# Experts taken in the order of their token counts, three of them with 64 slots and their weights standing

## Chip, cores and metric

One core of a Trainium2 chip runs the kernel. The time is device microseconds of one execution, the median of several. The parts of the core that matter here are TensorE (matmuls, with a weight load ahead of each), VectorE (DVE), ScalarE (ACT), the SP queue that issues the transfers from HBM, and 16 DMA engines that carry them out.

## What is computed

A stack of eleven mixing and feed-forward stages on 256 tokens of width 1024, and last a layer of eight routed experts and a norm. The experts, cut from the reference:

```python
def moe_swiglu(h, w_router, wg, wu, wd):
    xt = h.reshape(-1, d)                       # 256 x 1024
    logits = (xt @ w_router).astype(jnp.float32)
    top_v, top_i = lax.top_k(logits, TOP_K)     # 2 of 8
    gates = jax.nn.softmax(top_v, axis=-1)
    comb = jnp.sum(jax.nn.one_hot(top_i, N_EXPERTS) * gates[..., None], axis=1)
    y = jnp.zeros_like(xt)
    for e in range(N_EXPERTS):
        y = y + comb[:, e:e + 1] * swiglu(xt, wg[e], wu[e], wd[e])
    return y

def swiglu(x, wg, wu, wd):                      # 1024 x 3584, 1024 x 3584, 3584 x 1024
    return (jax.nn.silu(x @ wg) * (x @ wu)) @ wd
```

## The kernel before, in words

Weights come from HBM in raw tiles of 128 x 2048 floats (1 MiB), by `load` (line 431), one transfer on the SP queue each. `conv_w` (line 457) makes two halves of a tile and splits each half into two parts of a rounded type (fp32r): ScalarE casts the raw half to `whi` (line 462), VectorE subtracts it from the raw half and writes `wlo` (line 463). There are four buffers each of `whi` and `wlo` (`W_BUFS`), and 13 raw tiles in this stage (`RAW_BUFS` 4, `MORE_RAW` 6 and 3). Activations are split in the same way, and a product of two split operands is three matmuls (hi x hi, lo x hi, hi x lo), all issued by the helper `mm` (line 326).

`moe_stage` (line 1780) routes: VectorE finds each token's two experts, matmuls count the tokens ahead of each in its expert, and `sel` holds, for each token and expert, its slot counted from one, or zero. `rest` (line 1833) computes the gates `comb` and the largest count, later. Then `moe_round` (line 1877) runs over the eight experts in the order of their numbers. The tokens of an expert have 128 slots; if one has more than 128 tokens, a second round (line 1858) does the remaining ones.

`places` (line 1878) is called for a pair of experts: it compares slot numbers with `iota` to get the 0/1 matrix `pm`, and gathers the normed input of both experts by 32 matmuls (`mpg`), split into `gh` and `gl`. The first pair is gathered at the start, the others in group 3 of the odd experts. `places_back` (line 1904) transposes `pm` for the way back, in group 4 of each expert.

An expert runs over seven groups of 512 hidden columns (`NG`). In a group, `up` (line 1918) takes two raw tiles of `moe_g` and two of `moe_u`. The gathered tokens stand (`gh`, `gl`, a 128 x 128 block each) and the weights stream, 512 columns in a matmul: for gate (`eg`) and up (`eu`) 8 blocks of the input by three matmuls each. ScalarE takes the SiLU of `eg`, VectorE multiplies by `eu`, and `turn` (line 1939) transposes the 128 x 512 result by four TensorE transposes (`ept`) and splits it into `eah` and `eal`. `down` (line 1947) takes two raw tiles of `moe_d`; the turned activations stand, the weights stream, three matmuls of 512 columns for each of four blocks and two halves of the output (`eacc`). The down of a group is issued behind the up of the next one, and the turn between its gate and its up. After seven groups `back` (line 1963) weights the rows by their gates and scatters them to the tokens. The tile framework orders the instructions of each engine when the program is built; at run time each engine's queue is in order.

Of the kernel before, what the change touches and what calls it, by code (L numbers as in the profile page):

```python
# [10 lines left out]
F32 = mybir.dt.float32  # L11
# [18 lines left out]

STAGES = ["ssm", "xa0", "ffn0", "cf", "xa1", "ffn1", "ab", "cd", "hy0", "sw", "hy1", "moe", "final"]


# ---------------------------------------------------------------- host layout
# [196 lines left out]
# ---------------------------------------------------------------- device program  # L231
# [14 lines left out]
def hybrid_stack_kernel(ctx: ExitStack, tc: tile.TileContext, A, out, voff, coff, stages=STAGES):  # L246
# [5 lines left out]
    # the tiles of the stages; before the routed experts they make room for more raw weights  # L252
# [43 lines left out]
    # ---- allocation helpers  # L296
    def rotating(tag, shape, dt, name):
        # by turns in the pools that hold tiles of this kind
        c = turns[tag]
        i = c[0] % sum(n for _, n in c[1])  # L300
        c[0] += 1
        for pool, n in c[1]:
            if i < n:
                return pools[pool].tile(list(shape), dt, tag=tag, name=name, bufs=n)
            i -= n
# [7 lines left out]
    def g4(name, shape, dt=F32):  # L313
        return pools["attn" if "attn" in pools else "work"].tile(list(shape), dt, tag="g4", name=name, bufs=6)
# [16 lines left out]
    def early(name, shape, dt=F32, pool="work"):  # L331
        # kept until its pool ends
        return pools[pool].tile(list(shape), dt, tag="k_" + name, name=name, bufs=1)

    # ---- persistent data
# [17 lines left out]
    # constants used as they come, and those that are converted first  # L353
# [66 lines left out]
    # ---- weights  # L420
# [3 lines left out]
    def behind(insts):  # L424
        # keep what is traced inside from being issued before these
# [40 lines left out]
    def load_last(name, i):  # L466
        # in smaller steps, as nothing follows that could hide them
# [64 lines left out]
    def square_step(q, acc, m):  # L532
        # squares of the outputs as they end, and sums of the earlier ones
# [15 lines left out]
    class OutProj:  # L549
# [15 lines left out]
        def feed(self, hi, lo):  # L565
# [13 lines left out]
            if self.k == self.nk:  # L579
                # the two that come last lie in different banks  # L580
# [6 lines left out]
    # ---- norms  # L587
# [6 lines left out]
    def rsqrt(o, v):  # L594
        # o = v ** -0.5: a first guess from the bits of v, good to 3.5%, a step
        # of third order to 2.5e-5, and a Newton step to 1e-9
# [19 lines left out]
    def col_sums(o, parts, first=True, last=True):  # L616
        # sums over the partitions, one token per row: o [P, 2]
# [6 lines left out]
    def spread(o, c, start=False):  # L624
        # a value per token, from rows to every partition of o [., T]
# [21 lines left out]
    class Norm:  # L647
        # the input of a stage: gain times x in two parts; the root mean
        # square is known later and goes on what the products give
# [190 lines left out]
    def stack_hl(rows, n, dst):  # L840
        # rows: psum [n, W] -> dst [64, W] with the two parts on rows 0.. and 32..
# [3 lines left out]
    # ---- state-space mixer  # L845
    def ssm_stage():
# [20 lines left out]
        # time steps  # L867
# [25 lines left out]
        # minus the running sums; the first chunk's also as seen from the second  # L893
# [107 lines left out]
    # ---- cross attention  # L1001
# [126 lines left out]
    # ---- gated MLPs  # L1128
# [51 lines left out]
    # ---- convolution module  # L1180
    def cf_stage():
# [7 lines left out]
        def gate(w, o):  # L1189
            for b in range(2):  # L1190
# [7 lines left out]
                # twice the gated value; the halves are taken back below  # L1198
# [3 lines left out]
        def taps_pe(n):  # L1202
            # some of the taps, as products with diagonal matrices
# [82 lines left out]
    # ---- self attention on heads of 64  # L1286
    def head_stats(tiles, h):
        # tiles: [P, n, T], two heads on the partitions of each
# [17 lines left out]
    def head_scale(tiles, nq, gq, gk, st):  # L1306
        # unit-norm heads in place; both gains and the scale go on the keys
# [92 lines left out]
    def run_heads(n, score, turn, out, fill=(), a=LEAD):  # L1400
        # three steps per head, each behind the next head's earlier ones
# [16 lines left out]
    def ab_stage():  # L1418
# [3 lines left out]
        for part in range(2):  # L1422
# [5 lines left out]
            if part == 0:  # L1428
                # forget gate: negative log and its running sum
# [39 lines left out]
            def bias(hd):  # L1469
                def f(p):  # L1470
# [3 lines left out]
                    # the running sums are of the negated logs  # L1474
# [20 lines left out]
    def cd_stage():  # L1495
        h = begin()
        # differential half
# [62 lines left out]
        # sliding window half: query tile t holds heads t and t + 4  # L1560
# [65 lines left out]
    # ---- gated convolution and linear recurrence  # L1626
    def hybrid_stage(l):
# [6 lines left out]
        # the gate comes as half of one plus a tanh  # L1634
# [46 lines left out]
        # recurrence  # L1681
        ybs = []
        ss, la_, bb = [], [], []
        for i in range(4):
# [7 lines left out]
            # 1 - a^2 = -tanh(log a) (1 + a^2)  # L1692
# [394 lines left out]
```

## Time and profile before

| | |
|---|---|
| median of 3 runs | 2751.4 us (2750.27 to 2752.5) |
| span of the profiled execution | 2753.1 us |
| TensorE matmuls, busy | 2697.2 us, 98% of the span |
| weight loads, busy | 2398.0 us, 87% |
| VectorE, busy | 2201.6 us, 80% |
| ScalarE, busy | 1728.4 us, 63% |
| read from HBM | 616.04 MB, 224 GB/s over the span |
| expert tiles read | 112 of each of gate and up, and of down, 1 MiB each |

The span reaches from the first to the last instruction of one profiled execution; the times are of executions without the profiler, and the two differ by 1.7 us. Busy time of TensorE is modelled: matmuls overlap in the array, so the step from one start to the next is the better measure of what one costs. A weight load (PEld) has a duration of its own and runs beside the matmul before it. "Idle before" and the waits name what ended an engine's wait.

### The profile page before, as it was taken

The numbers are of one execution on the slowest core, as the hardware profiler recorded it, in microseconds if no ns is written. First come the engines' busy times: TensorE is split into PE (matmuls) and PEld (weight loads), VectorE is DVE, ScalarE is ACT, GpSimd is POOL, SyncE is SP. The second block draws the span as 40 slices with busy tenths as digits, with TensorE's granted clock in tenths as the row PEclk, the third lists the DMA queues.
The fourth block names the chain that finished last, engine by engine and source line by source line (L and its number), as shares of the span: only waits on it lengthen the run. The fifth ranks groups of instructions, "written<-read, shape, count | busy, mean of one in ns | idle before, by whom it ended". The sixth has DMA issues, their size and how long they took to land. (4 is left out here: it accounts for less than half of the span.)

```text
span 2753.1 us, 44558 instructions
## 1 busy us (share of the span) xinstructions
PE 2697.2 (98%) x17440; PEld 2398.0 (87%) x17440; DVE 2201.6 (80%) x3344; ACT 1728.4 (63%) x2563; POOL 7.7 (0%) x76
## 2 busy tenths in 40 slices
PE   8999999999999999999999999999999999999997
PEld 8799999999889988888999999888887878787876
DVE  8787597798668776767875577999998888888887
ACT  6665465565656555555654455877777777777776
POOL 0000000000000000000000000000000000000000
PEclk9999999999999999999999999999999999999999
DMA  7145445433435543342655554999999999999993
GB/s 260 62 169 184 138 155 189 162 108 123 169 117 190 184 145 127 113 139 100 260 198 184 184 177 169 347 363 351 351 343 343 339 349 359 349 344 343 362 343 115
DMA packets 87259, 620.05 MB, mean 225 GB/s; under 512 B 9936, under 2 KB 10064, under 8 KB 12800
## 3 DMA queue, kind: packets, MB, share of 16 engines
q1 hardware_dynamic: 86608, 616.57, 62.3%
q8 instruction: 138, 2.26, 0.3%
q14 instruction: 81, 0.66, 0.1%
q10 hardware_dynamic: 432, 0.56, 0.1%
HBM read 616.04 MB, written 1.05 MB: 224 GB/s over the span
## 5 line engine op out<-in xcount | busy, mean ns | idle before, releaser
L463 DVE TENSOR_TENSOR wlo<-raw,whi 128x1024 fp32r<-128x1024 f32 (+1 forms) x1164 | 1390.1, 1219 | 343.3 <-ACT whi L462 335.5
L462 ACT CAST whi<-raw 128x1024 fp32r<-128x1024 f32 (+1 forms) x1164 | 1195.6, 1049 | 573.8 <-PE wv L326 296.4
L326 PE MATMUL wv<-hh,whi 128*128 128x256 f32 x2400 | 681.2, 285 | 14.7 <-ACT hh L661 13.4
L326 PE MATMUL wv<-hl,whi 128*128 128x256 f32 x2400 | 680.1, 284 | 0.1
L326 PE MATMUL wv<-hh,wlo 128*128 128x256 f32 x2400 | 677.0, 283 | 1.6 <-DVE wlo L463 1.5
L326 PEld LDWEIGHTS wv<-hh,whi 128*128 128x128 f32 x2400 | 456.4, 190 | 18.7 <-ACT hh L661 14.6
L326 PEld LDWEIGHTS wv<-hh,wlo 128*128 128x128 f32 x2400 | 455.7, 190 | 4.1 <-DVE wlo L463 3.2
L326 PEld LDWEIGHTS wv<-hl,whi 128*128 128x128 f32 x2400 | 456.9, 190 | 1.8 <-DVE hl L662 0.7
L326 PE MATMUL eg<-wlo,gh 128*128 128x512 f32 x448 | 178.5, 398 | 2.8 <-DVE wlo L463 2.8
L326 PE MATMUL eu<-whi,gh 128*128 128x512 f32 x448 | 179.5, 401 | 0.0
L326 PE MATMUL eu<-wlo,gh 128*128 128x512 f32 x448 | 177.7, 397 | 1.4 <-DVE wlo L463 1.3
L326 PE MATMUL eg<-whi,gh 128*128 128x512 f32 x448 | 178.3, 398 | 0.0
L326 PE MATMUL eg<-whi,gl 128*128 128x512 f32 x448 | 177.2, 395 | 0.0
L326 PE MATMUL eacc<-whi,eal 128*128 128x512 f32 x448 | 177.1, 395 | 0.0
L326 PE MATMUL eacc<-whi,eah 128*128 128x512 f32 x448 | 177.0, 395 | 0.0
L326 PE MATMUL eu<-whi,gl 128*128 128x512 f32 x448 | 177.0, 395 | 0.0
L326 PE MATMUL eacc<-wlo,eah 128*128 128x512 f32 x448 | 162.6, 400 | 0.0
L326 PE MATMUL acc<-fl,whi 128*128 128x256 f32 x576 | 161.7, 281 | 0.0
L326 PE MATMUL acc<-fh,wlo 128*128 128x256 f32 x576 | 161.1, 280 | 0.0
L326 PE MATMUL acc<-fh,whi 128*128 128x256 f32 x576 | 160.6, 279 | 0.0
L837 DVE SCALAR_TENSOR_TENSOR cv<-pad,vec,cv 128x256 f32<-128x256 f32 x288 | 124.8, 479 | 1.4 <-ACT cv L834 0.6
L326 PEld LDWEIGHTS acc<-fl,whi 128*128 128x128 f32 x576 | 108.2, 188 | 0.3 <-DVE fl L478 0.3
(539 smaller groups left out, 4302.6 us busy)
## 6 DMA issues: line engine op xcount, KB each, us to landing
raw<-moe_u SPq DMA_DIRECT2D x112, 1024.0 KB, 7.1
raw<-moe_g SPq DMA_DIRECT2D x112, 1024.0 KB, 7.1
raw<-moe_d SPq DMA_DIRECT2D x111, 1024.0 KB, 7.0
raw<-ffn_in SPq DMA_DIRECT2D x44, 1024.0 KB, 5.0
raw<-sw_in SPq DMA_DIRECT2D x28, 1024.0 KB, 5.0
raw<-ffn_out SPq DMA_DIRECT2D x22, 1024.0 KB, 5.0
raw<-hy_in SPq DMA_DIRECT2D x20, 1024.0 KB, 5.0
raw<-ssm_in SPq DMA_DIRECT2D x18, 1024.0 KB, 5.2
```

The costliest lines, as they stand in the source:

```text
L326: return pe.matmul(o, l, r, start=start, stop=stop, skip_group_check=True)
L462: act.copy(hi[:, cs], raw[:, cs])
L463: dve.tensor_sub(lo[:, cs], raw[:, cs], f32v(hi[:, cs]))
L837: dve.scalar_tensor_tensor(y, pad[:, j, 4 - s : 4 + T - s], taps[i], y, op0=OP.mult, op1=OP.add)
```

## The change

- In `rest`, VectorE ranks experts 1 to 7 by their counts (expert 0 is given the first place by a large addend), writes the order into `idx`, and carries `sel`, the counts and `comb` over into that order (`selp`, `cp`, `combp`).
- Positions 0 to 7 take the ranks 0, 1, 5, 2, 3, 6, 4, 7. The positions with rank 5 and above, so the three with the fewest tokens among experts 1 to 7, have 64 slots, the others 128. The second round is entered if a count is above its slots.
- Expert 0's weights are addressed as before; the others' by an index that the SP queue reads from `idx` into a register, once per expert.
- The gather is done for the positions [0], [1, 2], [3, 4], [5, 6] and [7], five calls instead of four. For a 64-slot expert, `pm` holds the 64 slots twice, and hi and lo parts of the gathered tokens lie side by side in one 128-column operand `gx`.
- `up_small`: for gate and up the weights stand, a 128 x 128 block at a time, and the tokens stream: 128 columns (hi and lo) over `whi`, 64 columns (hi) over `wlo`. The two halves of the sum are added by ScalarE and VectorE; SiLU, product and split follow, and the result is already turned, so there is no `turn`.
- `down_small`: the operand of hi and lo (128 columns) stands and the weights stream, 512 columns, two matmuls instead of three. The scatter (`back`) is as before; `pb` adds both halves.

The diff, without comments and unchanged code:

```diff
 NE = 8

+RANKS = [0, 1, 5, 2, 3, 6, 4, 7]
+SMALL = 64
+CAPS = [P if r < 5 else SMALL for r in RANKS]
+GROUPS = [[0], [1, 2], [3, 4], [5, 6], [7]]
 STAGES = ["ssm", "xa0", "ffn0", "cf", "xa1", "ffn1", "ab", "cd", "hy0", "sw", "hy1", "moe", "final"]


 def _pack_in(w):
...
         return rotating("t2", shape, dt, name)

     def g4(name, shape, dt=F32):
-        return pools["attn" if "attn" in pools else "work"].tile(list(shape), dt, tag="g4", name=name, bufs=6)
+        if "attn" in pools:
+            return pools["attn"].tile(list(shape), dt, tag="g4", name=name, bufs=6)
+        return pools["work"].tile(list(shape), dt, tag="g4", name=name, bufs=5)

     def sm(name, shape, dt=F32):
...
             dve.tensor_add(comb, o1, o2)
-            cnt = keep.tile([P, 8], F32, name="cnt")
+            cnt = sm("cnt", (P, 8))
             dve.tensor_copy(cnt, pr[:, 0, 16:24])
+            key = sm("key", (P, 8))
+            dve.scalar_tensor_tensor(key, cnt, 8.0, iota8, op0=OP.mult, op1=OP.subtract)
+            dve.tensor_scalar(key[:, 0:1], key[:, 0:1], 8.0 * T + 16.0, 0.0, op0=OP.add, op1=OP.add)
+            kv = sm("kv", (P, 8))
+            dve.max(out=kv, in_=key)
+            ki = sm("ki", (P, 8), U32)
+            dve.max_index(ki, kv, key)
+            kf = sm("kf", (P, 8))
+            dve.tensor_copy(kf, ki)
+            idx = route["idx"] = keep.tile([P, 8], I32, name="idx")
+            oh = t1("oh", (P, 8, 8))
+            for j, r in enumerate(RANKS):
+                dve.tensor_scalar(oh[:, j, :], iota8, kf[:, r : r + 1], 0.0, op0=OP.is_equal, op1=OP.add)
+                dve.tensor_copy(idx[:, j : j + 1], kf[:, r : r + 1])
+            tmp = t1("ohm", (P, 8, 8))
+            cp = sm("cp", (P, 8))
+            for src, dst in ((sel[:, 0], selp[:, 0]), (sel[:, 1], selp[:, 1]), (cnt, cp), (comb[:, 0], combp[:, 0]), (comb[:, 1], combp[:, 1])):
+                dve.tensor_tensor(tmp, oh, bc2(src, 8), op=OP.mult)
+                dve.tensor_reduce(dst, tmp, axis=AX.X, op=OP.add)
+            for j, c in enumerate(CAPS):
+                dve.tensor_scalar(cp[:, j : j + 1], cp[:, j : j + 1], float(T - c), 0.0, op0=OP.add, op1=OP.add)
             mc = keep.tile([P, 1], F32, name="mc")
-            dve.tensor_reduce(mc, cnt, axis=AX.X, op=OP.max)
+            dve.tensor_reduce(mc, cp, axis=AX.X, op=OP.max)
             ci = keep.tile([P, 1], I32, name="ci")
...
             return ci

+        selp = keep.tile([P, 2, 8], F32, name="selp")
+        combp = keep.tile([P, 2, 8], F32, name="combp")
         ci = []
-        moe_round(0, hth, htl, sel, comb, lambda: ci.append(rest()))
-        most = nc.values_load(ci[0][0:1, 0:1], min_val=0, max_val=T)
-        with tc.If(most > P):
-            dve.tensor_scalar(sel, sel, -float(P), 0.0, op0=OP.add, op1=OP.add)
-            moe_round(1, hth, htl, sel, comb)
+        moe_round(0, hth, htl, sel, selp, combp, lambda: ci.append(rest()))
+        most = nc.values_load(ci[0][0:1, 0:1], min_val=0, max_val=2 * T)
+        with tc.If(most > T):
+            for j, c in enumerate(CAPS):
+                dve.tensor_scalar(selp[:, :, j : j + 1], selp[:, :, j : j + 1], -float(c), 0.0, op0=OP.add, op1=OP.add)
+            moe_round(1, hth, htl, selp, selp, combp)

     def xtok(t, n):
         return xT.rearrange("p k t -> p (k t)")[:, (2 * t + n) * 512 : (2 * t + n + 1) * 512]

     def x_by_tokens():
...
             act.copy(xtok(i // 2, i % 2), px[i])

     ss = keep.tile([P, 2, 2], F32, name="ss")

-    def moe_round(rnd, hth, htl, sel, comb, rest=None):
-        def places(ep):
-            pm = [t1("pm", (P, 2, P), F32R) for _ in range(2)]
+    def moe_round(rnd, hth, htl, sel0, sel, comb, rest=None):
+        regs = {}
+        def fetch(raw, src, e, i, cs=slice(0, 2048)):
+            if e not in regs:
+                regs[e] = None
+                if e:
+                    regs[e] = nc.values_load(
+                        route["idx"][0:1, e : e + 1], engines=[mybir.EngineType.SP], min_val=0, max_val=NE - 1
+                    )
+            if e:
+                w = A[src][bass.ds(regs[e], 1), i : i + 1, :, cs].rearrange("a b p n -> (a b p) n")
+            else:
+                w = A[src][0, i][:, cs]
+            nc.sync.dma_start(raw[:, cs], w)
+        def load_e(src, e, i):
+            raw = raw_tile()
+            fetch(raw, src, e, i)
+            return [conv_w(raw[:, j * 1024 : (j + 1) * 1024]) for j in range(2)]
+        def load_e_last(src, e, i):
+            raw = raw_tile()
+            r = []
+            for j in range(2):
+                cs = slice(j * 1024, j * 1024 + 1024)
+                fetch(raw, src, e, i, cs)
+                r.append(conv_w(raw[:, cs], 1 + j))
+            return r
+        def places(es):
+            w = len(es) * P
+            pm = [t1("pm", (P, T), F32R) for _ in range(2)]
             for t in range(2):
-                for u in range(2):
-                    e = 2 * ep + u
-                    dve.tensor_scalar(pm[t][:, u, :], iota, sel[:, t, e : e + 1], 0.0, op0=OP.is_equal, op1=OP.add)
-            gh = [g4("gh", (P, KD, P), F32R) for _ in range(2)]
-            gl = [g4("gl", (P, KD, P), F32R) for _ in range(2)]
+                for u, e in enumerate(es):
+                    c = CAPS[e]
+                    dve.tensor_scalar(
+                        pm[t][:, u * P : u * P + P].rearrange("p (a b) -> p a b", b=c),
+                        bc2(iota[:, :c], P // c), (sel if e else sel0)[:, t, e : e + 1], 0.0, op0=OP.is_equal, op1=OP.add,
+                    )
             pgs = []
...
                     for t in range(2):
-                        r = pm[t].rearrange("p u s -> p (u s)")
-                        mm(pg[:, j, :], hth[2 * t + k // 4][:, cs], r, j == 0 and t == 0, False)
-                        mm(pg[:, j, :], htl[2 * t + k // 4][:, cs], r, False, j == 1 and t == 1)
+                        r = pm[t][:, :w]
+                        mm(pg[:, j, :w], hth[2 * t + k // 4][:, cs], r, j == 0 and t == 0, False)
+                        mm(pg[:, j, :w], htl[2 * t + k // 4][:, cs], r, False, j == 1 and t == 1)
                 pgs.append(pg)
-            for u in range(2):
+            r = []
+            for u, e in enumerate(es):
+                c = CAPS[e]
+                gx = [g4("gx", (P, KD, P), F32R) for _ in range(2 if c == P else 1)]
                 for k2 in range(4):
                     ks = slice(2 * k2, 2 * k2 + 2)
-                    split(pgs[k2][:, :, u * P : (u + 1) * P], gh[u][:, ks, :], gl[u][:, ks, :])
-            return [(2 * ep + u, gh[u], gl[u], [None, None], pm, u) for u in range(2)]
+                    o = u * P
+                    hi = gx[0][:, ks, :c]
+                    lo = gx[1][:, ks, :] if c == P else gx[0][:, ks, c:]
+                    act.copy(hi, pgs[k2][:, :, o : o + c])
+                    dve.tensor_sub(lo, pgs[k2][:, :, o + P - c : o + P], f32v(hi))
+                r.append((e, gx, [None, None], [p[:, u * P : u * P + P] for p in pm], c == P))
+            return r

         def places_back(x):
-            e, pm, u = x[0], x[4], x[5]
+            e, pm = x[0], x[3]
             pb = t1("pb", (P, T), F32R)
...
             for t in range(2):
-                pe.transpose(pt[:, 0, t * P : (t + 1) * P], f32v(pm[t][:, u, :]), ident)
+                pe.transpose(pt[:, 0, t * P : (t + 1) * P], f32v(pm[t]), ident)
             for t in range(2):
-                mm(pt[:, 1, :8], f32v(pm[t][:, u, :]), comb[:, t, :], False, t == 1)
+                mm(pt[:, 1, :8], f32v(pm[t]), comb[:, t, :], False, t == 1)
             act.copy(pb, pt[:, 0, :])
...
             dve.tensor_copy(g, pt[:, 1, e : e + 1])
-            x[3][:] = [pb, g]
+            x[2][:] = [pb, g]

         def up(x, g, mid):
-            e, gh, gl = x[:3]
+            e, (gh, gl) = x[:2]
             po = [wv("eg"), wv("eu")]
...
                 for c in range(2):
-                    wt = load(src, (e, 2 * g + c))
+                    wt = load_e(src, e, 2 * g + c)
                     for k4 in range(4):
...
             return a

+        def up_small(x, g, mid):
+            e, (gx,) = x[:2]
+            n = CAPS[e]
+            s = []
+            for i, src in enumerate(("moe_g", "moe_u")):
+                if i and mid:
+                    mid()
+                po = wv(("eg", "eu")[i]).rearrange("p a b -> p (a b)").rearrange("p (m s) -> p m s", m=4)
+                for c in range(2):
+                    wt = load_e(src, e, 2 * g + c)
+                    for k4 in range(4):
+                        k = 4 * c + k4
+                        whi, wlo = wt[k4 // 2]
+                        for m in range(4):
+                            cs = slice((k4 % 2) * 512 + m * P, (k4 % 2) * 512 + (m + 1) * P)
+                            mm(po[:, m, :], whi[:, cs], gx[:, k, :], k == 0 and m == 0, False)
+                            mm(po[:, m, :n], wlo[:, cs], gx[:, k, :n], False, k == KD - 1 and m == 3)
+                s.append(pools["work"].tile([P, 4, n], F32, tag="eas", name="eas", bufs=3))
+                act.copy(s[i], po[:, :, n:])
+                dve.tensor_add(s[i], s[i], po[:, :, :n])
+            act.activation(s[0], s[0], AF.Silu)
+            dve.tensor_mul(s[0], s[0], s[1])
+            ax = t2("eax", (P, 4, P), F32R)
+            split(s[0], ax[:, :, :n], ax[:, :, n:])
+            return ax
         def turn(a):
...
             for c in range(2):
-                end = e == NE - 1 and g == NG - 1 and c == 1
-                wt = (load_last if end else load)("moe_d", (e, 2 * g + c))
+                wt = load_e("moe_d", e, 2 * g + c)
                 for j in range(2):
...
                         mm(acc[n], ah[:, f], wlo[:, cs], False, g == NG - 1 and c == 1 and j == 1)

+        def down_small(x, g, a, acc):
+            e = x[0]
+            for c in range(2):
+                end = e == NE - 1 and g == NG - 1 and c == 1
+                wt = (load_e_last if end else load_e)("moe_d", e, 2 * g + c)
+                for j in range(2):
+                    whi, wlo = wt[j]
+                    for n in range(2):
+                        cs = slice(n * 512, (n + 1) * 512)
+                        mm(acc[n], a[:, 2 * c + j, :], whi[:, cs], g == 0 and c == 0 and j == 0, False)
+                        mm(acc[n], a[:, 2 * c + j, :], wlo[:, cs], False, g == NG - 1 and c == 1 and j == 1)
         def back(x, acc):
-            pb, gs = x[3]
+            pb, gs = x[2]
             yh = [t2("eyh", (P, 512), F32R) for _ in range(2)]
...
                         act.activation(t2("fsq", (P, 512)), xtok(t, n), AF.Square, accum_out=ss[:, t, n : n + 1])

-        todo = places(0)
+        def step_down(late):
+            x, g, a, acc = late
+            if acc is None:
+                acc = [ps("eacc", (P, 512)) for _ in range(2)]
+            (down if x[4] else down_small)(x, g, a, acc)
+            if g == NG - 1:
+                back(x, acc)
+                acc = None
+            return acc
+        def turned():
+            if late and late[0][4]:
+                late[2] = turn(late[2])
+        todo = places(GROUPS[0])
         late = None
...
             for g in range(NG):
-                f = (lambda: late.__setitem__(2, turn(late[2]))) if late else None
-                a = up(x, g, f)
+                a = (up if x[4] else up_small)(x, g, turned)
                 if rest and e == 0 and g == 0:
...
                 if late is not None:
-                    y, gg, aa, ac = late
-                    if ac is None:
-                        ac = [ps("eacc", (P, 512)) for _ in range(2)]
-                    down(y, gg, aa, ac)
-                    acc = ac
-                    if gg == NG - 1:
-                        back(y, ac)
-                        acc = None
+                    acc = step_down(late)
                 late = [x, g, a, acc]
-                if g == 3 and e % 2 and e < NE - 1:
-                    todo += places((e + 1) // 2)
+                if g == 3 and not todo and e < NE - 1:
+                    todo += places(next(q for q in GROUPS if q[0] == e + 1))
                 if g == 4:
                     places_back(x)
-        y, gg, aa, ac = late
-        down(y, gg, turn(aa), ac)
-        back(y, ac)
+        turned()
+        step_down(late)

     def final_stage():
```

## Rows read from the trace of the kernel before

**Rows 1.** Windows: us; busy us (count) of PE, PEld, DVE, ACT, POOL; clock, DMA, GB/s.

```profile
...
2250.00:2375.00 125.00, 124.09 (x550) 99.33 (x549) 110.16 (x108) 91.91 (x101) 0.00 (x0) 1.00 0.95 355
...
sum 875.00, PE 871.20 PEld 701.54 DVE 778.58 ACT 655.05 POOL 0.00; mean PE 124.46 PEld 100.22 DVE 111.23 ACT 93.58 POOL 0.00
...
```

**Rows 2.** Waits from 1800 to 2750: waiter, releaser, total us, times, longest.

```profile
...
ACT eah L477 <- PE ept L1942: 71.2, 39, 2.7
...
ACT whi L462 <- PE eg L326: 35.0, 90, 1.7
...
PEld eg L326 <- DVE wlo L463: 5.6, 8, 1.0
...
PEld eu L326 <- DVE wlo L463: 4.0, 6, 0.7
...
```

**Rows 3.** The same for the SP queue, which issues the transfers, from 1750.

```profile
...
SPq L435 <- DVE wlo L463: 784.0, 303, 6.6
...
```

**Rows 4.** Instructions on mpt: minimum, median, maximum ns, first and last start.

```profile
...
L1910 PEld LDWEIGHTS mpt<-direct,pm x16: 139/141/143, 1812.5 to 2678.6; 128*128 128x128 f32 x16
...
```

**Rows 5.** Timeline of TensorE: start, us, and what; one group of an expert.

```profile
...
2011.50 0.40 PE L326 MATMUL eg<-whi,gh 128*128 128x512 f32 x1
...
2016.87 0.40 PE L326 MATMUL eg<-wlo,gh 128*128 128x512 f32 x1
...
2017.77 0.39 PE L326 MATMUL eu<-whi,gl 128*128 128x512 f32 x1
...
```

**Rows 6.** Timeline of weight loads before the gather.

```profile
...
1718.31 1.31 PEld L326 LDWEIGHTS ms<-ones,sq 128*128 128x128 f32 x11
...
```

**Rows 7.** Timeline of TensorE in three other stretches.

```profile
...
19.93 0.28 PE L326 MATMUL wv<-hh,whi 128*128 128x256 f32 x1
...
23.45 0.28 PE L326 MATMUL wv<-hh,whi 128*128 128x256 f32 x1
...
1120.75 0.38 PE L326 MATMUL sc<-i2n,st 128*128 128x128 f32 x2
1120.97 0.34 PE L326 MATMUL sc<-maskb,identb 128*128 128x384 bf16 x1
...
1728.39 0.50 PE L326 MATMUL eg<-whi,gh 128*128 128x512 f32 x1
...
```

**Rows 8.** Groups by line and form: weight loads, whole kernel; count, busy us, mean ns.

```profile
...
L326 PEld LDWEIGHTS eg<-whi,gh 128*128 128x128 f32 x448 | 84.2, 188 | 19.4
...
L326 PEld LDWEIGHTS <-identb 128*128 128x128 bf16 x40 | 3.8, 95 | 6.1 <-issue 5.9
...
```

**Rows 9.** Groups by line and form, 1800 to 2750.

```profile
...
L463 DVE TENSOR_TENSOR wlo<-raw,whi 128x1024 fp32r<-128x1024 f32 x622 | 731.5, 1220 | 65.0 <-ACT whi L462 61.4
L462 ACT CAST whi<-raw 128x1024 fp32r<-128x1024 f32 x621 | 629.8, 1051 | 83.5 <-PE eg L326 35.0 <-PE eacc L326 26.5 <-PE eu L326 18.3
...
L478 DVE TENSOR_TENSOR eal<-ept,eah 128x512 fp32r<-128x512 f32 x53 | 36.3, 685 | 11.4 <-ACT eah L477 11.4
...
L478 DVE TENSOR_TENSOR gl<-mpg,gh 128x256 fp32r<-128x256 f32 x24 | 9.7, 420 | 3.3 <-ACT gh L477 3.0
...
```

**Rows 10.** Timeline of VectorE: the old comb, and short operations of the end.

```profile
...
1742.34 0.17 DVE L1845 TENSOR_TENSOR comb<-o,o 128x16 f32<-128x16 f32 x1
...
2745.25 0.16 DVE L600 TENSOR_TENSOR rcs<-rcs,rvs 128x2 f32<-128x2 f32 x1
2745.45 0.17 DVE L601 TENSOR_SCALAR rcs<-rcs 128x2 f32<-128x2 f32 x1
...
```

**Rows 11.** Windows of 5 us, columns as in rows 1.

```profile
...
1720.00:1725.00 5.00, 4.95 (x43) 4.20 (x40) 4.34 (x25) 2.33 (x4) 0.00 (x0) 1.00 0.84 303
...
345.00:350.00 5.00, 3.54 (x15) 3.25 (x16) 4.93 (x14) 3.04 (x7) 0.00 (x0) 0.50 0.00 0
...
```

**Rows 12.** Timeline of TensorE in the second of these windows.

```profile
...
347.42 0.41 PE L326 MATMUL wv<-hh,wlo 128*128 128x256 f32 x1
347.63 0.41 PE L326 MATMUL wv<-hh,whi 128*128 128x256 f32 x1
...
```

## The prediction

> **What bounds the kernel now.** The change touches only the routed experts, the stretch from about 1720 us to the end, so I read that stretch and not the page's shares. First the windows over it [rows 1]: of 875 us TensorE is busy in 871, VectorE in 779, ScalarE in 655, and the transfers hold their engines at 0.95. Columns near full do not say which sets the pace; the waits do [rows 2]. ScalarE's conversions wait for matmuls (whi for eg, for one) because the four buffers of converted weights are full, while TensorE's loads wait for converted weights only 5.6 + 4.0 us in 950. The queue of transfers likewise waits 784 us for raw buffers that VectorE has yet to release [rows 3], and nothing in the list waits for a transfer. So TensorE is last, and conversion and transfer have slack behind it. One expert takes 123.7 us: the transposes of its slot places come once per expert, the first at 1812.5 and the eighth at 2678.6, seven periods [rows 4].
>
> Within that, the stream of matmuls is regular [rows 5]: from 2011.50 to 2016.87 there are 23 steps, 0.2335 us for each 512-column matmul. The turn of the activations costs 2017.77 - 2016.87 - 2 x 0.2335 = 0.43 us on TensorE.
>
> **The change, part by part.** The routing counts, worked out from the reference's inputs, are 58, 42, 99, 63, 66, 73, 32, 79 for experts 0 to 7. Expert 0 goes first with 128 slots; the 64-slot ones are those with 63, 42 and 32 tokens. They fit, so the second round stays out. Three of eight experts change form.
>
> *Small experts on TensorE.* A large expert issues 7 x 2 x 8 x 3 = 336 matmuls for gate and up and 168 for down, all of 512 columns. A small one issues 112 of 512 columns for down. So 392 x 0.2335 = 91.5 us leave, and seven turns, 3.0 us. For gate and up come 7 x 2 x 8 x 4 x 2 = 896 matmuls of 128 and 64 columns, each with a new 128-column block of weights standing. In columns this would be half of before; but each needs its own weight load. What a load costs when almost nothing is streamed is shown by eleven 128x128 loads for one-column products (col_sums): (1.31 - 0.19) / 10 = 0.112 us each [rows 6]. The nearest relatives of the new stream are two products on loads of the same rounded type, of 128 and 256 columns: they start at 1120.75, and the next starts at 1120.97, 0.11 us each; products of 256 columns, where load and product are about even, step 30 times from 19.93 to 23.45, 0.117 us [rows 7]. Going below 128 columns buys nothing, then. I take 0.112, the longest run of loads; bounds 0.110 and 0.117. So 896 x 0.112 = 100.4 us come, 94.5 go: +5.9 us per small expert, +17.6 for three (bounds +12 and +31).
>
> *Its cover.* Conversion does not bind: 84 halves at 731.5 / 622 = 1.18 us of VectorE [rows 9] are 99 us; the two additions, the product and the split that replace the two steps of 0.685 us come to about 1.5 us a group (0.42 for 128x256 from PSUM; I take 0.35 for each of the two from SBUF) and the rest of an expert to some 4, so about 113 us against 129.6 on TensorE.
>
> *Where a small expert can stall.* The old rhythm is even: 6 x 0.2335 = 1.40 us of TensorE per converted half, 1.22 us to convert it [rows 5, 9]. The new one is not: 16 x 0.112 = 1.79 us per half in gate and up, 4 x 0.2335 = 0.93 in down. In down TensorE eats four buffered halves in 3.7 us, while a freed buffer takes 1.05 + 1.22 us to refill. If conversions stand ahead of the copy and addition of the sums, the first half of the next group is about 0.2 us late. If they stand behind them, they queue behind an instruction that waits for TensorE: the addition ends about 0.8 us after the last up product, then come the halves at 1.22 us; 1.1 + 0.3 + 0.3 us lost in down, 1.0 at the next gate, 0.2 at the next up, 2.9 us a group. The trace of before has ScalarE wait at the turn in this way, 71.2 us in 39 waits [rows 2], with hardly a wait of TensorE behind it; so I choose nearer the lower end, 0.8 us a group, 17 us for 21 groups (bounds 4 and 61).
>
> *One more gather.* There are five groups of places instead of four; the last has one expert. Its 32 products of 128 columns are load-bound, 32 x 0.112 = 3.6 us, on TensorE's path. The first gather has half the columns but the same 32 loads and gains nothing on TensorE; two masks and eight small splits move from the stage's start to group 3 of expert 0, worth -1 us at the start (0 to -2).
>
> *Ranking.* About 39 short VectorE operations come in one chain. Short ones step by 0.20 us [rows 10]: 7.8 us. VectorE has some 5 us of slack in 50 [rows 1], and two or three converted halves cover 3 to 4 us; I take +3 us (0 to 8). If that cover were gone the whole 7.8 us would be TensorE's.
>
> *Transfers.* All 336 tiles are still fetched, by addresses read from a register. The SP queue waits for the expert's index before that expert's first tile; queued behind are the next tiles, and behind these ScalarE and VectorE. The old comb stands at 1742.3 [rows 10], so the index is due by about 1751; the 43rd tile is issued when the 30th has been used, 30 x 2.95 us after the first product at 1728.4 [rows 7], at about 1817. The seven register reads I price at 0: 13 raw tiles of 2.95 us stand ahead of each. A read that took longer than these 38 us would be TensorE's from there on. Small experts ask for tiles more slowly than large ones, so no new contention.
>
> *Tail.* The last expert becomes a small one; the scatter and the last norm are as before: 0.
>
> The sum: 17.6 + 17 + 3.6 - 1 + 3 = +40 us. The profiled execution spans 2753.1 us against a median of 2751.4, so 2793 in a profile and about **2791** by the median. Bounds: 12 + 4 + 3.6 - 2 + 0 = +18 and 31 + 61 + 3.6 + 8 = +104: 2769 to 2855.
>
> **The rivals.** *Faster: loads do hide.* If load and short product together stepped well below 0.105 us (94.5 / 896, the point from which it decides), TensorE would drop under conversion, and a small expert would take VectorE's 113 us plus some waiting for ScalarE, about 115. Three times -8.7, and +6 for gather and ranking: 2731. For it: only the columns. Against it: none of these runs steps faster than 0.11 [rows 6, 7], and a load of this type lasts 188 ns where a bfloat16 one lasts 95 [rows 8]. I leave it 0.10. The Trainium skill, "TensorE: Matmul & The Clock Gate", section "Back-to-back issue gap", gives about 81 ns per 128-column product in a sustained stream of load and product; by it gate and up would take 896 x 0.081 = 73 us, an estimate from that page, and this rival would come true. The trace disagrees, 110 to 112 ns.
>
> *Slower by more: the queues' order.* The worst order above, 2.9 us a group, adds 44 us to the forecast: 2835. Chance 0.15.
>
> *The clock.* TensorE is granted 1.00 through the experts. Around 346 us, after waits between two stages, it was granted 0.50, the lower level of 1.2 GHz [rows 11], and 256-column products stepped 0.21 us instead of 0.117 [rows 12]. If the short products made it fall, 896 x 0.10 + 112 x 0.23 = 115 us more per small expert: about 3135. Against it: the short products from 1720 to 1725 ran at 1.00 [rows 11]. Chance 0.04.
>
> *It doesn't do what it says.* If the second round were entered, another pass over eight experts, some 1000 us. The fullest small expert has 63 of 64 slots. Chance 0.01.
>
> **How the numbers follow.** The forecast 0.64, the bad order 0.15, loads that hide 0.10, terms that cancel to within 0.2% (about 5.5 us, what a measurement of this kernel can tell) 0.06, clock 0.04, second round 0.01. Slower: 0.64 + 0.15 + 0.04 + 0.01 = 0.84. The range holds nearly all of the forecast's case and most of the bad order's, and reaches below the lower bound for the cancelling case: 2757 to 2845.
>
> **What would show it.** Gate and up of a small expert: loads back to back at 0.11 us, products of 64 columns spaced like those of 128. Its period about 130 us plus TensorE's waits for wlo, which are the order's price; large ones still 123.7; the transfers' share lower in small ones. A step of 0.08 us would make the forecast wrong in sign.

## The result, and the profile of the changed kernel

The changed kernel takes 2972.38 us (median; 2970.83 to 2974.82) against 2751.42 us before: a ratio of 1.080, with a 95% interval from 1.079 to 1.082. It is 221 us slower. The forecast had the sign (2791 us) but not the size: the time lies far above its range of 2757 to 2845. What happened is what the prediction had listed as the rival "the clock" and given a chance of 0.04, though it put that rival at 3135 us.

The page of the changed kernel shows it in one row, the granted clock of TensorE in 40 slices of the span. In the kernel before, all 40 digits are 9.

```profile
span 2969.6 us, 48369 instructions
...
PE 2911.9 (98%) x18900; PEld 2661.1 (90%) x18900; DVE 2226.7 (75%) x3426; ACT 1753.7 (59%) x2605; POOL 7.7 (0%) x76
...
PEclk9999999999999999999999999986699986689666
```

Three dips, one for each small expert. Windows over the experts (columns as in [rows 1], which they answer) put them in place: large experts from 1800 to 1950 and from 2175 to 2400, small ones in the 225 us between and after, and at the end.

```profile
1800.00:1950.00 150.00, 150.00 (x667) 120.99 (x666) 137.41 (x130) 116.22 (x123) 0.00 (x0) 1.00 0.95 357
1950.00:2175.00 225.00, 224.54 (x1169) 210.15 (x1168) 139.64 (x149) 118.73 (x144) 0.00 (x0) 0.69 0.65 234
2175.00:2400.00 225.00, 223.72 (x1005) 180.59 (x1004) 206.32 (x202) 173.64 (x190) 0.00 (x0) 1.00 0.93 352
2400.00:2625.00 225.00, 224.72 (x1140) 210.56 (x1139) 137.05 (x141) 116.84 (x137) 0.00 (x0) 0.67 0.65 235
...
2725.00:2975.00 250.00, 228.99 (x1147) 213.22 (x1145) 144.03 (x160) 119.94 (x146) 0.00 (x0) 0.68 0.46 166
```

In the first two small experts TensorE is busy throughout (224.5 and 224.7 of 225 us) at a granted clock of 0.69 and 0.67, and in the last one, whose row also holds the end of the kernel, at 0.68. VectorE, ScalarE and the transfers fall to two thirds of what they do in large experts, where VectorE and the transfers are near their limits. So they follow TensorE. Its waits from 1950 us on, which answer [rows 2], are next to nothing (waiter, releaser, total us, times, longest):

```profile
PE eu L334 <- DVE wlo L471: 2.3, 2, 1.1
PE eacc L334 <- DVE eax L486: 1.3, 1, 1.3
PE mpg L334 <- DVE gx L1974: 0.8, 2, 0.6
```

The timeline of TensorE where the first small expert begins (start, duration, what) shows the fall itself. The last 512-column product of the large expert starts at 1963.34, the first short one at 1963.57.

```profile
1963.34 0.39 PE L334 MATMUL eacc<-wlo,eah 128*128 128x512 f32 x1
1963.57 0.22 PE L334 MATMUL eg<-gx,whi 128*128 128x128 f32 x1
...
1963.71 0.31 PE L334 MATMUL eg<-gx,whi 128*128 128x128 f32 x1
...
1969.96 0.30 PE L334 MATMUL eg<-gx,whi 128*128 128x128 f32 x1
1970.11 0.29 PE L334 MATMUL eg<-gx,wlo 128*128 128x64 f32 x1
1970.22 0.46 PE L334 MATMUL eg<-gx,whi 128*128 128x128 f32 x1
1970.47 0.36 PE L334 MATMUL eg<-gx,wlo 128*128 128x64 f32 x1
1970.64 0.45 PE L334 MATMUL eg<-gx,whi 128*128 128x128 f32 x1
```

From 1963.71 to 1969.96 lie 28 pairs of a product over whi and one over wlo, (1969.96 - 1963.71) / 56 = 0.1116 us a product: the 0.112 that the prediction took from [rows 6]. At 1970.1 everything becomes about half as fast, and a pair takes 0.42 us instead of 0.223. The weight loads slow down as well. Here they are at the fifth fall of this expert, 2089.6: they last 0.33 us instead of 0.19, and start 0.21 us apart instead of 0.11.

```profile
2089.42 0.19 PEld L334 LDWEIGHTS eu<-gx,wlo 128*128 128x128 f32 x1
2089.53 0.24 PEld L334 LDWEIGHTS eu<-gx,whi 128*128 128x128 f32 x1
2089.65 0.34 PEld L334 LDWEIGHTS eu<-gx,wlo 128*128 128x128 f32 x1
2089.87 0.33 PEld L334 LDWEIGHTS eu<-gx,whi 128*128 128x128 f32 x1
2090.08 0.33 PEld L334 LDWEIGHTS eu<-gx,wlo 128*128 128x128 f32 x1
```

It does not stay down. In each group the clock comes back during the down product, which still streams 512 columns, and falls again in gate and up. Windows of 3 us over one group (clock third from the right):

```profile
2051.00:2054.00 3.00, 3.00 (x29) 3.00 (x29) 2.96 (x4) 1.78 (x3) 0.00 (x0) 1.00 0.88 333
2054.00:2057.00 3.00, 3.00 (x23) 3.00 (x22) 1.92 (x3) 1.65 (x2) 0.00 (x0) 0.75 0.92 333
2057.00:2060.00 3.00, 3.00 (x16) 3.00 (x15) 1.05 (x2) 1.32 (x2) 0.00 (x0) 0.50 0.93 350
...
2072.00:2075.00 3.00, 3.00 (x9) 2.42 (x9) 1.74 (x3) 2.36 (x3) 0.00 (x0) 0.50 0.00 0
2075.00:2078.00 3.00, 3.00 (x13) 2.42 (x13) 2.82 (x4) 2.37 (x3) 0.00 (x0) 0.84 0.76 265
2078.00:2081.00 3.00, 3.00 (x29) 3.00 (x27) 2.59 (x5) 2.28 (x6) 0.00 (x0) 1.00 0.92 292
```

The reader should see that TensorE is busy 3.00 us of 3.00 on both sides of the fall. The 512-column products that start at 2072 step at 0.43 us until 2075.6 and at 0.23 us from there. 0.50 is the lower level, 1.2 GHz.

**The sum by these rows.** In the first small stretch a mean of 0.69 between 1.00 and 0.50 is 2 x 0.31 x 225 = 139.5 us at the lower level. What runs there takes about 1.9 times as long (0.42 for 0.223, 0.43 for 0.233), so 139.5 x (1 - 1/1.9) = 66 us are lost. The second gives 70 in the same way. The third has 160 us at the lower level; about 10 of these belong to the kernel's last norm (from 2957 us on no product is left, and the granted clock is 0.62 up to the end at 2969.6), so 150 and 71. Together that is an estimate of 207 us. What the short products cost at the full clock, 3 x (896 x 0.1116 - 94.5) = 16 us, makes it 223, and 221 were measured.

### The profile page after: what moved, and what is told of

Read it like the earlier page. It is cut to its first block, busy times and chain, and to the rows that moved or that the text cites. A ratio compares the mean times of both kernels' runs of the same rounds, so it can differ in the third digit from the quotient of the medians.

```text
span 2969.6 us, 48369 instructions
## 1 busy us (share of the span) xinstructions
PE 2911.9 (98%) x18900; PEld 2661.1 (90%) x18900; DVE 2226.7 (75%) x3426; ACT 1753.7 (59%) x2605; POOL 7.7 (0%) x76
## 5 line engine op out<-in xcount | busy, mean ns | idle before, releaser
L334 PE MATMUL eu<-gx,whi 128*128 128x128 f32 x672 | 285.7, 452 | 0.0
L334 PE MATMUL eu<-gx,wlo 128*128 128x64 f32 x672 | 242.3, 361 | 0.0
L334 PEld LDWEIGHTS eu<-gx,wlo 128*128 128x128 f32 x672 | 222.8, 332 | 0.0
L334 PEld LDWEIGHTS eu<-gx,whi 128*128 128x128 f32 x672 | 222.6, 331 | 0.0
L334 PE MATMUL eg<-whi,gx 128*128 128x512 f32 x560 | 179.7, 400 | 0.0
L334 PE MATMUL eg<-gx,whi 128*128 128x128 f32 x672 | 178.8, 334 | 0.0
L334 PE MATMUL eu<-whi,gx 128*128 128x512 f32 x560 | 178.5, 399 | 0.0
L334 PE MATMUL eg<-gx,wlo 128*128 128x64 f32 x672 | 170.8, 270 | 0.0
L334 PEld LDWEIGHTS eg<-gx,wlo 128*128 128x128 f32 x672 | 149.5, 222 | 1.1
L334 PEld LDWEIGHTS eg<-gx,whi 128*128 128x128 f32 x672 | 148.1, 220 | 1.2
```

Source lines behind the costliest of these rows:

```text
L334: return pe.matmul(o, l, r, start=start, stop=stop, skip_group_check=True)
```

## The experiments

Theory A: short products by themselves bring the clock down. Rival B: the loads are slow in themselves in such a stream, by contention with transfers and conversion or by their order, and the clock is a side effect.

**e_twice: the same loads, more columns.** The tokens are streamed twice (a broadcast operand), so that each load of a small expert's gate and up is followed by 256 columns. Nothing is left out; a product of two low parts and a copy nobody reads are added. The sum lies in two banks of the accumulators (PSUM) and is read out in two parts instead of one. Cut to the products:

```diff
...
-mm(po[:, m, :], whi[:, cs], gx[:, k, :], ...)
-mm(po[:, m, :n], wlo[:, cs], gx[:, k, :n], ...)
+d = po[m // 2][:, m % 2, :].rearrange("p (r s) -> p r s", r=2)
+mm(d, whi[:, cs], bc2(gx[:, k, :]), ...)
+mm(d, wlo[:, cs], bc2(gx[:, k, :]), ...)
...
```

> Gate and up of a small expert keep their 896 weight loads, but every product streams 256 columns: the operand of 128 columns twice over, with both halves of the sum in two PSUM banks; the second copy is not used, and wlo is multiplied with the low parts too. Theory A (the products are so short that TensorE's granted clock falls): more columns keep the clock at 1.00, pairs step about 0.117 us as the 256-column ones do elsewhere in this kernel, a small expert takes about 134 us plus some waits, and the whole 2785 to 2805 us, some 170 less than the changed kernel although TensorE streams 2.7 times the columns in gate and up. Theory B (loading these blocks is slow in itself, 0.21 us each): the loads are the same 896, so 2970 us or more.

Measured: 2780.55 us, a ratio of 1.010 (1.008 to 1.012). More than twice the columns in gate and up, and 192 us faster than the change. That is 4 us below the range of theory A, and far from the 2970 of B. The window from 2000 to 2050, and the groups of the up product in the change and in e_twice (durations minimum/median/maximum in ns, first and last start):

```profile
2000.00:2050.00 50.00, 50.00 (x378) 47.61 (x377) 41.59 (x51) 37.14 (x51) 0.00 (x0) 1.00 0.89 328
```

```profile
L334 PEld LDWEIGHTS eu<-gx,whi x672: 192/333/337, 1971.8 to 2941.3; 128*128 128x128 f32 x168
L334 PE MATMUL eu<-gx,whi x672: 304/454/455, 1971.8 to 2941.4; 128*128 128x128 f32 x168
```

```profile
L334 PEld LDWEIGHTS eu<-gx,whi x672: 187/188/193, 1973.1 to 2752.4; 128*128 128x128 f32 x168
L334 PE MATMUL eu<-gx,whi x672: 277/281/367, 1973.2 to 2752.5; 128*128 128x256 f32 x168
```

The loads are the same in number, tiles and order, and take 188 ns instead of 333 in the median: B falls. On TensorE only the products behind them differ, and the clock stays at 1.00. The 30 us that remain are what the steps say: 3 x (896 x 0.117 - 94.5) = 31.

**e_lo128 and e_lo128b: one product of the pair widened.** The product over wlo streams all 128 columns instead of 64 (it too adds the product of the low parts). e_lo128b is the same program once more.

```diff
-mm(po[:, m, :n], wlo[:, cs], gx[:, k, :n], ...)
+mm(po[:, m, :], wlo[:, cs], gx[:, k, :], ...)
```

> The product on wlo streams all 128 columns instead of 64 (the low parts times wlo are added too). Loads unchanged, columns up from 96 to 128 a load. Theory A: at the full clock nothing is lost, as a load hides 128 columns (0.111 us a pair), and the clock holds longer or always: between 2790 (always) and 2970 us. Theory B: unchanged, 2970 us.

> The kernel whose wlo product streams 128 columns instead of 64, once more with more rounds; one execution of it gave 2770 us and the profiled one 2784 us with a single low stretch of 27 us behind a wait of TensorE. Theory A (at 128 columns the products lie close to what holds the clock up, and whether it falls is decided by small waits): the executions scatter between 2765 and 2790 us, in steps of 10 to 15 us, a step for each low stretch. Rival B (the 14 us belong to the profile): all executions within 3 us of 2770.

Measured: e_lo128 2783.87 in the profiled execution and 2770.09 in the other; e_lo128b 2770.97 (2769.15 to 2771.53, four executions), a ratio of 1.0068 (1.0051 to 1.0085). All lie far from B's 2970 and a little below 2790, the lower bound of theory A for e_lo128. The same stretch of the first small expert, in the profiled execution of the one and of the other:

```profile
2025.00:2050.00 25.00, 23.45 (x187) 22.33 (x187) 22.20 (x27) 17.60 (x24) 0.00 (x0) 1.00 0.94 343
2050.00:2075.00 25.00, 25.00 (x120) 25.00 (x119) 9.47 (x12) 8.35 (x12) 0.00 (x0) 0.50 0.44 159
2075.00:2100.00 25.00, 25.00 (x180) 23.10 (x180) 19.61 (x22) 18.66 (x23) 0.00 (x0) 0.95 0.76 274
```

```profile
2025.00:2050.00 25.00, 23.45 (x191) 22.60 (x190) 21.35 (x27) 16.92 (x26) 0.00 (x0) 1.00 0.93 343
2050.00:2075.00 25.00, 25.00 (x209) 24.23 (x208) 19.54 (x23) 17.30 (x23) 0.00 (x0) 1.00 0.78 284
```

64 more columns on every second product keep the clock up nearly always. In the profiled execution of e_lo128 it fell for 27 us, from 2049.9 to 2077.2. The mean granted clock of that execution is 0.987; that of the other five is 0.991 or 0.992, which leaves no room for such a fall. Windows of 2.5 us show short falls besides, of about 3.5 us each: one in e_lo128 at 2572, two in e_lo128b at 2557.5 and 2748.5.

The long fall came 1 us after a wait of TensorE of 1.55 us, ahead of the second half of a gather, but the execution without it has that same wait. So the wait does not decide it alone, and what tipped the one execution is open. Of the two expectations for e_lo128b, B has the right numbers (all within 2 us of 2771) but not the right reason, since the profiled execution of e_lo128b, at 2770.76, is no slower than the others. A's scatter was seen only in the profiled execution of e_lo128.

The 19.4 us of e_lo128b over the kernel before are what short products cost with the clock nearly always up: 16 by the step of 0.1116, some 3 by its 7 us at the lower level.

**e_two: one small expert fewer.** The last position gets 128 slots and the old form; the small experts at the third and sixth place stay.

```diff
-CAPS = [P if r < 5 else SMALL for r in RANKS]
+CAPS = [P if r < 5 or r == 7 else SMALL for r in RANKS]
```

> The two small experts at the third and sixth place keep the change's form; the one at the last place has 128 slots and the form of before. Theory A (the clock falls under the short products of each small expert by itself): two thirds of the loss, 2751 + 2/3 x 221 = 2898 us, low granted clock (about 0.6 over windows of 25 us) inside these two experts alone and 1.00 in the last one. Rival B (the loss builds up over the round, or sits at its end, where no large expert follows): the two small ones that large experts follow cost much less than the last one, and the time comes out under 2860 us.

Measured: 2900.2 us (2896.8 and 2903.6), a ratio of 1.054 (1.052 to 1.056), where A had 2898. The two small stretches and the end:

```profile
1950.00:2175.00 225.00, 224.55 (x1168) 210.91 (x1167) 139.47 (x149) 118.43 (x144) 0.00 (x0) 0.69 0.65 236
...
2400.00:2625.00 225.00, 224.74 (x1140) 210.80 (x1139) 137.13 (x140) 116.30 (x135) 0.00 (x0) 0.67 0.64 235
2625.00:2875.00 250.00, 246.52 (x1100) 198.37 (x1099) 224.03 (x212) 188.70 (x203) 0.00 (x0) 0.99 0.79 300
```

The two that large experts follow cost two thirds of the 221 us, so the last one costs the remaining third: rival B, under 2860 us, is out.

**e_all128: everything but the small form.** All experts get 128 slots and the old gate, up, turn and down; the ranking, the order, the register addresses and the five gathers stay.

```diff
-SMALL = 64
+SMALL = P
-        return pools["work"].tile(..., tag="g4", name=name, bufs=5)
+        return pools["work"].tile(..., tag="g4", name=name, bufs=6)
```

> All positions have 128 slots and the old form; the order by counts, the five gathers, the ranking on VectorE and the addresses from a register stay. Theory A, with the prediction's terms for these (3.6 + 3 - 1): 2752 to 2762 us. If one of them (the register reads, above all) carries part of the loss: more than 2775 us.

Measured: 2750.77 us (ten executions), a ratio of 0.9996 (0.9986 to 1.0006): these parts together cost nothing that can be measured. The time lies 1 us below the expected range. The rival of more than 2775 us is out.

**e_mix: the same work in another order.** Half of the down product of the group before is issued between gate and up of a small expert, which halves the stretches of short products.

```diff
+        def halfway():
+            turned()
+            if late and not late[0][4]:
+                ...
+                down_small(late[0], late[1], late[2], late[3], (0,))
+                early_c.append(1)
...
-up_small(x, g, turned)
+up_small(x, g, halfway)
...
-down_small(x, g, a, acc)
+down_small(x, g, a, acc, (1,) if early_c else (0, 1))
```

> The same products, loads and transfers as the change, in another order: half of the down product of the group before (512 columns a product) stands between gate and up of a small expert, so that the stretch of short products is halved and wide products come twice as often between them. Theory A (the clock falls some time after the short products begin and comes back under wide ones, so that the length of a short stretch counts): a smaller share of the small experts at the low clock, a time between 2776 and 2900 us. Rival B (only the mean load of the small experts counts, not how the products are ordered): the same as the change, 2960 to 2985 us. Rival C (each short stretch, however short, ends at the low clock and each return to full clock costs the same time again): slower than the change, over 2990 us.

Measured: 2945.9 us (2943.93 and 2947.87), a ratio of 1.071 (1.068 to 1.073): 26 us of the 221 come back. Its first two small stretches, and then three windows of 25 us in the last expert:

```profile
1950.00:2175.00 225.00, 224.23 (x1216) 206.39 (x1216) 150.86 (x161) 128.17 (x155) 0.00 (x0) 0.74 0.70 254
...
2400.00:2625.00 225.00, 223.59 (x1191) 205.29 (x1190) 151.00 (x156) 126.63 (x147) 0.00 (x0) 0.73 0.70 250
```

```profile
2800.00:2825.00 25.00, 25.00 (x111) 24.23 (x111) 11.21 (x10) 8.99 (x11) 0.00 (x0) 0.50 0.52 185
2825.00:2850.00 25.00, 25.00 (x103) 23.45 (x102) 12.52 (x14) 10.59 (x13) 0.00 (x0) 0.50 0.53 184
2850.00:2875.00 25.00, 25.00 (x111) 24.12 (x111) 10.88 (x12) 9.31 (x11) 0.00 (x0) 0.50 0.35 125
```

None of the three numbers came. The order counts, against B, since the same work is 26 us shorter; C has the wrong sign; and A, which let me hope for under 2900, has the direction but not the size. In two experts the mean clock rises from 0.69 and 0.67 to 0.74 and 0.73. In the last it stays at 0.50 from 2800 to 2875, although eight 512-column products stand between gate and up there as well: half as long a wide stretch brings the clock back in some places and not in others. What decides between these was not settled.

**v_stand: the tokens stand instead.** If short products behind many loads are the fault, the small experts need the opposite layout: hi and lo parts of 64 tokens stand side by side as one 128-column operand, and the weights stream, 512 columns a product, two products instead of three. The two halves of the sum are added and turned by one product with two stacked identities.

```diff
-for m in range(4):
-    mm(po[:, m, :], whi[:, cs], gx[:, k, :], ...)
-    mm(po[:, m, :n], wlo[:, cs], gx[:, k, :n], ...)
+mm(po, gx[:, k, :], whi[:, cs], k == 0, False)
+mm(po, gx[:, k, :], wlo[:, cs], False, k == KD - 1)
...
+def turn_small(r):
+    ...
+    mm(pt[:, i, m, :], r[i][:, m * P : (m + 1) * P], fold, ...)
```

> Small experts keep 64 slots with both parts side by side, but the tokens stand and the weights stream, 512 columns, two matmuls instead of three for gate, up and down; a product with two stacked identities turns the result and adds the halves. TensorE then needs 123.7 - 0.2335 x (112 + 56) - 3.0 + 12.5 = 94 us a small expert at the full clock. Theory A: no short products beyond some 2 us a group, clock 1.00, the small experts wait for conversion (VectorE about 110 us), about 115 us each: 2725 to 2745 us. Were the clock's fall due to TensorE having slack as such, it would fall here too and the time would stay above 2751.

Measured: 2703.37 us (2700.96 to 2705.5), a ratio of 0.982 (0.980 to 0.984): faster than both kernels, by some 47 us and by 269. The first small expert's windows:

```profile
1950.00:2000.00 50.00, 48.91 (x226) 38.72 (x225) 47.61 (x47) 41.73 (x48) 0.00 (x0) 1.00 0.94 362
2000.00:2050.00 50.00, 47.60 (x238) 36.49 (x236) 47.56 (x56) 42.84 (x59) 0.00 (x0) 1.00 0.98 385
2050.00:2100.00 50.00, 48.49 (x207) 35.04 (x208) 46.70 (x47) 41.38 (x50) 0.00 (x0) 1.00 1.00 403
```

The clock is 1.00 and TensorE is no longer alone at its limit: VectorE is busy 47.6 of 50 us and the transfers' share reaches 1.00. TensorE's weight loads now wait for VectorE, from 1800 us on (5.6 and 4.0 us in the kernel before [rows 2]):

```profile
PEld eg L334 <- DVE wlo L471: 34.5, 64, 1.1
PEld eu L334 <- DVE wlo L471: 23.3, 56, 1.1
```

A small expert now takes 47 / 3 = 16 us less than a large one, some 108 us, which is near the time of its conversion, 99 us of VectorE for the halves alone by the prediction's count: three of every nine wide products are gone, and conversion now shares in setting the pace. I had expected 2725 to 2745, with more waiting between conversion and products than there was.

## Why the prediction was wrong, point by point

- **What bounds it** was right. TensorE set the pace before, and it does so after, more than ever.
- **The step of the small experts** was right: 0.112 us forecast, 0.1116 measured at full clock, which makes 16 us of the 17.6. A pair of 128 and 64 columns takes as long as one of 128 and 128 (0.223 us in the change and in e_lo128b). With the clock nearly always up the whole costs 19.4 us (e_lo128b), beside the +40 of the sum. So the sign that came true rests on less than a tenth of the loss.
- **The stalls** of 17 us (bounds 4 to 61) were over-priced. e_lo128b leaves next to nothing for them; TensorE waits 2.2 + 1.8 + 1.7 + 1.1 us from 1950 us to the end there. The worst order of the queues, the rival at 2835, did not come.
- **Gather, ranking and start**, forecast at 3.6 + 3 - 1 = 5.6 us, measured -1.1 us with an interval from -3.9 to +1.7 (e_all128). The register reads were free, as forecast.
- **The clock** is the step that failed, and more than the whole size of the error: the sum has nothing for it, and it cost about 207 us, while the other terms were some 21 too high. The prediction took the granted clock to stay at 1.00; in the small experts it was 0.67 to 0.69. The mechanism stood in the text with the right cause, but its chance was judged by one row: 1720 to 1725 us at a clock of 1.00 [rows 11]. That row could not speak against it. In the changed kernel, too, the short products run at 1.00 at first, from 1963.57 to 1970.1, longer than that whole window, and only then does the clock fall. The other row at hand, 345 to 350 us at 0.50, I explained by waits, and so took waits for the condition; TensorE's waits in the small experts are under 5 us in all, and the clock is low for some 440.
- **Its price** was too high in the other direction: 115 us per small expert supposed that all of it ran at the lower level. Some 146 us of each do, at a loss of 69, because the 512-column down product brings the clock back in every group. The rival's 3135 lies 163 us above the measured time, nearly as far as the forecast's 2791 lies below it.
- **The rival "loads do hide"** is out: no run shows a mean step below 0.111.

The Trainium skill, "TensorE: Matmul & The Clock Gate", section "HAM oscillation — how this bites in real kernels", has the clock fall where the engine idles between groups of matmuls, waiting for transfers. By that rule this kernel would have kept its clock. The trace disagrees: TensorE is busy 3.00 us of 3.00 in the windows around the fall, with its products evenly spaced, and the clock is 0.50 all the same. The measurement decides.

## What to carry to other kernels

As this kernel shows, a tile layout with fewer columns need be no saving when each product brings its own weight load, and it can cost far more than the loads: before trading wide products for many short ones, look for a row where such a stream runs as long as the new one will, and where there is none, price the lower clock as a main case. Where a product can be laid out either way, try the larger operand streaming and the small one standing; here that turned +8% into -1.8%. And if such a stream must stay, wider products can be faster than narrow ones.

## What the runs showed that I had not expected

- The granted clock of TensorE fell from 1.00 to 0.50 with the engine busy all the time, under pairs of 128- and 64-column products with a load each (0.223 us a pair, then 0.42). With pairs of 128 and 128 columns it fell for long in one execution of six (and for 3.5 us at a time in both profiled ones), with pairs of 256 in neither of the two executions.
- Weight loads follow that clock: 188 to 192 ns at 1.00, 333 at 0.50.
- More work took less time: 64 unneeded columns on every second short product made the kernel 201 us faster.
